# One table that fixes the order of four engines from the last output projection products to the first FFN products, with new PSUM banks

## The chip, the cores and the metric

The kernel runs on one core of a Trainium2 chip. The metric is device time in microseconds (us) for one execution, the median over runs. A core has five instruction streams that work side by side and wait for each other by semaphores: TensorE (PE, matrix products), VectorE (DVE), ScalarE (ACT), GpSimd (POOL) and SyncE (SP), which here issues most of the DMA loads. Products land in PSUM, which this kernel uses as eight banks of 128 x 512 floats; everything else lives in SBUF.

## The reference: what is computed

One layer of a hybrid decoder on x of 1024 tokens by 1024 features, float32:

```python
h = rms_norm(x, mix_norm)
z = h @ w_in                     # split into the parts of two head groups
o_gla = rms_norm(gla_chunked(...), gla_norm) * silu(gr)     # gated linear attention
o_swa = swa_sink_attention(...)                             # sliding window
x = x + concatenate([o_gla, o_swa]) @ w_out
h2 = rms_norm(x, ffn_norm)
u = causal_dwconv(h2 @ w_up, conv_w, conv_b)                # w_up: 1024 x 5632
a, b = split(u, 2)
return x + (silu(a) * b) @ w_down                           # w_down: 2816 x 1024
```

The place of the change is the middle: the output projection with `w_out`, the second RMSNorm, and the first products with `w_up`.

## The kernel before, in words

**Tiles and products.** The 1024 tokens are eight tiles of 128 (t = 0 to 7). Float32 products are made of two parts: every operand is split into a high part (`hi`, a cast by ACT) and a low part (`lo`, the rest, by a subtraction on DVE or POOL; `split`, L102), and three passes (hi·hi, hi·lo, lo·hi) are added up. The output projection and the FFN products use the Winograd form of Strassen's method: the 2 x 2 block product needs seven block products, P1 to P7, instead of eight, at the price of sums and differences of the blocks. One such product, for a pair of tiles (output projection, `o_product`, L829) or for a chunk of 128 columns on each side (FFN, `product`, L977), is 4 x 3 = 12 matmuls of 128 x 128 by 128 x 512 into one bank. P3 of the output projection adds onto the bank of P1, and P4 of the pairs 2 and 3 onto that of P7.

**The stretch of the change.** In order of time:
1. The last gated tiles are transposed into banks called ogt (`gate_tr`, L676, last reader L695); the output projection runs P1 for the pairs i = 0 to 3, then P7 (0, 1), P6 and P5, and then P2, P3, P4 and the rest of P7 mixed. DVE adds each finished bank to the residual tiles `acc` (`o_adds`, L844, its DVE line L852).
2. RMSNorm2 of a tile t whose sums are complete: ACT squares and sums (`norm2_stat`, L214), DVE makes the mean and POOL a power (`rms_scale`, L174); the rows are scaled (`norm2_rows`, L224), either by ACT (scale) and POOL (weights) for the tiles in ROWS_POOL, or by DVE alone in one instruction per half (L235). PE transposes the tile (eight 128 x 128 transposes; L286 for tiles 0 to 3, L253 for 4 to 7). Tiles 0 to 3 are then split into `big` (hi on ACT L290, lo on DVE L298). Tiles 4 to 7 go through `norm2_sums` (L256), which makes the blocks B22, T1, T2, T3 and T4 of the seven products in five sums and splits each.
3. The FFN goes over 22 chunks; chunk c has seven products, with weights that are loaded by SP (`load_side`, L909), combined (`first_sums` L928, `sums` L923) and split (`up_operand`, L934; A11, A12, A22 and S1 to S4 are its operands). The first product needs the high and low parts of tiles 0 to 3, and its matmuls run the eight with high parts first and the four with low parts last. `post` (L1072) puts convolution and gate behind the products; `down_pair` (L1161) multiplies with `w_down`.

**What sets the order.** Every step is registered with a time (`at(time, function, ...)`, `at_us`), the steps are emitted in the order of those times, and a scheduler then orders each engine's instructions by its own estimate. O, TU and the like are starts of stages. Only PE is pinned to the order of emission, by manual dependencies from O to TU + 0.07 (end of the function). On DVE, ACT and POOL the scheduler decides, within what data and buffers demand; a step wrapped in `behind` is put later by it. A norm tile's sums (`norm2_sums`) are one step of about 15 instructions, and so is a tile's scaling.

**PSUM.** Two pools, "a" and "b", of four banks each. `bank` (L55) picks a pool by the beginning of a name, and in turns where no name fits (the ogt banks are such); in a pool the banks go round. A new tile of a bank waits for the last reader of the one before it. All eight FFN banks (`fb0` to `fb3`, `gb0` to `gb3`) are opened at one time, by `open_up_banks` (L750). The FFN product of chunk 0 goes to `gb`, those of the other chunks to `fb`; tiles 3 and 7 of the norm are transposed into `fb2` and `fb3`.

Of the kernel before, what the change touches and what calls it, by code (L numbers as in the profile page):

```python
# [17 lines left out]
P = 128  # L18
# [10 lines left out]
SUMS, EA, EB = 2.01, -25, -14  # L29
# [5 lines left out]
def hymba_layer_kernel(ctx, tc, x, mix_norm, w_in, w_alpha2, b_alpha, gla_norm,  # L35
# [178 lines left out]
    def norm2_stat(t):  # L214
        pn, acc = fin["pn"], fin["acc"][t]
        ss = pn.tile([P, 1], F32, tag="n2ss", name=f"n2ss_{t}", bufs=2)
        if t == 7:
            fin["h", t] = pn.tile([P, D], F32, tag="n2h", name=f"n2h_{t}", bufs=2)
        act.activation(fin["h", t] if t == 7 else early_raw(), acc, AF.Square, accum_out=ss)
        fin["r", t] = rms_scale(ss, D, 1, f"n2{t}", pn, "n2")  # L220

    ROWS_POOL = (0, 1, 2, 4, 5)

    def norm2_rows(t):  # L224
        acc, r = fin["acc"][t], fin["r", t]
# [3 lines left out]
        if t in ROWS_POOL:
            for c in halves:  # L230
                act.activation(h[:, c], acc[:, c], AF.Copy, scale=r[:, 0:1])
                pool.tensor_mul(h[:, c], h[:, c], fin["ffn"][:, c])
            return
        for c in halves:
            dve.scalar_tensor_tensor(h[:, c], acc[:, c], r[:, 0:1], fin["ffn"][:, c],  # L235
                                     op0=ALU.mult, op1=ALU.mult)

    def norm2_tr(t):
        h = fin["h", t]
        if t < 4:  # L240
            b11 = fin["b11"] = fin["pn"].tile([P, 4, 2, P // 2], F32, tag="b11", name=f"b11_{t}", bufs=1)
            tr_hi(t, 0, h, "n2", True)
            act.copy(b11, trs["n2", t, 0])
            tr_lo(t, 0, "n2", True)
            tr_hi(t, 1, h, "n2", True)
            tr_lo(t, 1, "n2", True)
            return
        pbs = fin["pb", t] = []
        for q in range(2):
            pt = bank(f"n2pt_{t}_{q}")  # L250
            for k in range(4):
                c = (q * 4 + k) * P
                pe.transpose(pt[:, k * P:(k + 1) * P], h[:, c:c + P], ident)  # L253
            pbs.append(pt.rearrange("p (k c h) -> p k h c", k=4, h=2))

    def norm2_sums(t):  # L256

        i, ex = t - 4, fin["ex"]
        p0, p1 = fin["pb", t]

        def put(src, dst, eng=dve):
            dst = dst.rearrange("p k r (h c) -> p k r h c", h=2)
            split(src, dst[:, :, 0], dst[:, :, 1], eng)

        b12 = fin["h", t][:, 0:512].rearrange("p (k h c) -> p k h c", k=4, h=2)
        b11 = fin["b11"]
        b21 = big[:, i, 4:8].bitcast(F32).rearrange("p k r (h c) -> p k r h c", h=2)
        act.copy(b12, p0)
        put(p1, big[:, t, 4:8])
        dve.tensor_sub(p1, p1, b12)  # L270
        put(p1, ex[1][:, i])
        dve.tensor_sub(p0, p0, b11)
        put(p0, big[:, t, 0:4])
        dve.tensor_add(p1, p1, b11)
        put(p1, ex[0][:, i])
        dve.tensor_sub(p0, b21[:, :, 0], p1)
        dve.tensor_add(p0, p0, b21[:, :, 1])
        put(p0, ex[2][:, i])
# [550 lines left out]
    def o_product(name, i):  # L829
        onto = "P1" if name in ("P6", "P5", "P3") else "P7" if name == "P4" and i > 1 else None  # L830
        if onto is None:
            psb["o", name, i] = bank(f"o{name}_{i}")
        pb = psb["o", onto or name, i]
        left = o_left(name, i)
        for k in range(4):
            for n, (ra, rb) in enumerate(PASSES):
                pe.matmul(pb, lhsT=left[:, k, ra, :], rhs=two_streams(ow[name, k][:, rb, :]),
                          start=(onto is None and k == 0 and n == 0), stop=(k == 3 and n == 2),
                          skip_group_check=onto is not None)
# [348 lines left out]
    def last_row(t):  # L1188
# [166 lines left out]
    for k in range(4):  # L1355
# [17 lines left out]
    for n, (name, i) in enumerate((("P2", 0), ("P3", 0), ("P4", 0), ("P2", 1), ("P3", 1), ("P7", 2), ("P4", 1), ("P2", 2),  # L1373
                                   ("P3", 2), ("P4", 2), ("P2", 3), ("P3", 3), ("P7", 3), ("P4", 3))):
        u = O + 7 + 0.5 * n
        at(u, o_product, name, i)
        if name in ("P3", "P4"):
            t = i + 4 if name == "P4" else i
            at(u + 0.005, norm2_rows, t)
    for t, n in ((0, 20), (4, 21), (1, 22), (5, 24), (2, 26), (6, 27), (3, 28)):  # L1380
        at(O + 0.5 * n - 0.002, norm2_tr, t)
        if t > 3:
            at(O + 0.5 * n + 0.01, norm2_sums, t)
# [123 lines left out]
```

## Time and profile before

| | us |
|---|---|
| median of 3 runs | 1007.57 (1007.51 to 1008.27) |
| the profiled execution | 1006.84 |
| its span, first to last instruction | 1005.1 |
| PE busy | 975.3 |
| DVE busy | 818.4 |
| POOL busy | 649.2 |
| ACT busy | 505.8 |
| mean granted clock of TensorE | 0.991 |

The span is divided among the engines by "busy"; several are busy at once. A timeline row reads: start, duration, engine, line, operation, output <- inputs, shapes, count, and in brackets the idle time before it with the instruction that ended it. A row of waits reads: who waits <- for whom, total us, times, longest. A row of windows gives for each engine its busy time and its instructions, and then the granted clock of TensorE (1.00 is full speed). Matmuls overlap in the pipe, so that the distance between two starts, and not the duration, is what a product costs.

### The profile page before, as it was taken

To read this page: it belongs to the slowest core of one execution; us is meant where nothing else is said; L and a number is where in the kernel's file an instruction comes from. 1 tells how busy PE (TensorE), PEld (TensorE's weight loads), DVE (VectorE), ACT (ScalarE), POOL (GpSimd) and SP (SyncE) were. 2 spreads that over 40 slices of the span, in tenths; PEclk is the share of its full clock that TensorE was granted. 3 is DMA by queue.
4 is the path that set the end of the run, shared out by engine and by line. 5 is a ranking of instruction groups with operands and counts; after the bars stand their busy time and mean duration, and the time that the engine had idled before them with its cause. 6 is when DMAs were issued, how large, how long until landed. Compare 5 with 4: busy or idle time off the path is not lost.

```text
span 1005.1 us, 13939 instructions
## 1 busy us (share of the span) xinstructions
PE 975.3 (97%) x4915; PEld 842.7 (84%) x4915; DVE 818.4 (81%) x1363; ACT 505.8 (50%) x1039; POOL 649.2 (65%) x542
## 2 busy tenths in 40 slices
PE   8999999999989996999999999999999999999998
PEld 6898878888878774888888888888888888888887
DVE  6877668767573677698998989898989999898986
ACT  5637655445452374455454555445454545455451
POOL 5592232325572654577978788888878797888760
PEclk9999999999998997999999999999999999999999
DMA  6152123032304102202122221212121212222104
GB/s 224 64 157 66 46 64 84 22 85 64 105 1 170 40 0 64 74 32 63 42 64 63 64 64 43 84 43 84 35 72 41 63 42 64 63 64 63 42 22 168
DMA packets 67540, 68.23 MB, mean 68 GB/s; under 512 B 4650, under 2 KB 52237, under 8 KB 67470
## 3 DMA queue, kind: packets, MB, share of 16 engines
q1 hardware_dynamic: 63484, 62.35, 20.1%
q10 hardware_dynamic: 3986, 4.99, 2.1%
q8 instruction: 39, 0.64, 0.3%
q14 instruction: 31, 0.25, 0.1%
HBM read 58.41 MB, written 4.19 MB: 62 GB/s over the span
## 4 chain that ended last, share of the span: by engine, by line
PE 55%; DVE 5%; POOL 2%; issue 1%; DMA 0%; ACT 0%; POOLq 0%; ACTq 0%
PE fb L990 35%; PE dn_P L1171 17%; PE dl L1200 1%; PE fb L1200 1%; DVE n2h L235 1%; PE gb L990 1%; DVE acc L1175 1%; DVE ua L997 0%; DVE ex L107 0%; DMA up<-in_w_up_dram 0%; POOL dw L107 0%; DVE acc L852 0%; DVE big L107 0%; DVE big L298 0%; ACT ex L104 0%
## 5 line engine op out<-in xcount | busy, mean ns | idle before, releaser
L1171 PE MATMUL dn_P<-dw,dg 128*128 128x512 f32 x840 | 205.0, 381 | 1.1 <-DVE acc L1175 0.7
L1175 DVE TENSOR_TENSOR acc<-acc,dn_P 128x1024 f32<-128x1024 f32 x140 | 169.3, 1210 | 31.3 <-PE dn_P L1171 31.2
L1171 PEld LDWEIGHTS dn_P<-dw,dg 128*128 128x128 f32 x840 | 157.2, 189 | 27.1 <-DVE acc L1175 3.2
L107 POOL TENSOR_TENSOR dw<-dn,dw 128x512 fp32r<-128x512 f32 x50 | 64.5, 1290 | 35.8 <-ACT dw L104 35.8
L997 DVE SCALAR_TENSOR_TENSOR ua<-fb,cc,ua 128x511 f32<-128x511 f32 (+1 forms) x84 | 61.9, 739 | 1.2 <-ACT ua L1002 0.8
L990 PE MATMUL fb<-big,A11w 128*128 128x512 f32 x252 | 58.3, 380 | 1.1 <-ACT e L1046 1.1
L990 PE MATMUL fb<-big,S1w 128*128 128x512 f32 x252 | 58.6, 379 | 0.0
L990 PE MATMUL fb<-big,S4w 128*128 128x512 f32 x252 | 58.1, 379 | 0.0
L990 PE MATMUL fb<-big,A12w 128*128 128x512 f32 x252 | 58.1, 379 | 0.0
L990 PE MATMUL fb<-ex,S2w 128*128 128x512 f32 x252 | 58.0, 379 | 0.0
L990 PE MATMUL fb<-ex,A22w 128*128 128x512 f32 x252 | 57.8, 379 | 0.0
L990 PE MATMUL fb<-ex,S3w 128*128 128x512 f32 x252 | 57.8, 379 | 0.0
L522 POOL TENSOR_TENSOR pr<-pr,sm 128x512 f32<-128x512 f32 x16 | 17.3, 1078 | 60.5 <-DVE sm L521 34.6
L1002 ACT ACTIVATE ua<-fb,cc 128x512 f32<-128x512 f32 x42 | 32.7, 778 | 46.3 <-DVE fb L1050 30.0
L990 PEld LDWEIGHTS fb<-big,A11w 128*128 128x128 f32 x252 | 47.5, 189 | 8.2 <-ACT e L1046 1.5
L990 PEld LDWEIGHTS fb<-big,A12w 128*128 128x128 f32 x252 | 47.6, 189 | 6.8
L990 PEld LDWEIGHTS fb<-big,S1w 128*128 128x128 f32 x252 | 47.6, 189 | 6.8
L990 PEld LDWEIGHTS fb<-ex,S3w 128*128 128x128 f32 x252 | 47.6, 189 | 6.8
L990 PEld LDWEIGHTS fb<-big,S4w 128*128 128x128 f32 x252 | 47.6, 189 | 6.8
L990 PEld LDWEIGHTS fb<-ex,A22w 128*128 128x128 f32 x252 | 47.6, 189 | 6.8
L990 PEld LDWEIGHTS fb<-ex,S2w 128*128 128x128 f32 x252 | 47.6, 189 | 6.8
L107 POOL TENSOR_TENSOR A22w<-up,A22w 128x512 fp32r<-128x512 f32 x22 | 30.0, 1363 | 32.0 <-ACT A22w L104 32.0
(487 smaller groups left out, 2573.7 us busy)
## 6 DMA issues: line engine op xcount, KB each, us to landing
up<-in_w_up_dram SPq DMA_DIRECT2D x44, 512.0 KB, 3.8
dn<-in_w_down_dram SPq DMA_DIRECT2D x22, 512.0 KB, 3.4
acc<-in_x_dram SPq DMA_DIRECT2D x8, 512.0 KB, 4.8
out_dram<-acc SPq DMA_DIRECT2D x15, 256.0 KB, 2.1
xt<-in_x_dram SPq DMA_DIRECT2D x7, 512.0 KB, 3.3
vraw<-in_w_in_dram SPq DMA_DIRECT2D x4, 512.0 KB, 4.4
graw<-in_w_in_dram SPq DMA_DIRECT2D x4, 512.0 KB, 3.6
qt<-qt ACTq DMA_DIRECT2D x16, 128.0 KB, 2.2
```

Source lines behind the costliest of these rows:

```text
L107: (eng or pool).tensor_sub(lo, src, hi.bitcast(F32))
L235: dve.scalar_tensor_tensor(h[:, c], acc[:, c], r[:, 0:1], fin["ffn"][:, c], op0=ALU.mult, op1=ALU.mult)
L522: pool.tensor_tensor(pr, pr, den[:, hs].rearrange("p (j o) -> p j o", o=1).broadcast_to((P, 4, P)), ALU.mult)
L990: pe.matmul(pb, lhsT=w[:, ra, k, :], rhs=b_operand(bn, k, rb).rearrange("p t (h c) -> p t c h", h=2), start=(onto is None and i == 0), sto ...
L997: dve.scalar_tensor_tensor(dst, src, w, dst, op0=ALU.mult, op1=ALU.add)
L1002: act.activation(u[:, a:z], y[:, a:z], AF.Identity, bias=b, scale=w2)
L1171: pe.matmul(pb[:, i], lhsT=g[:, ra, c:c + P], rhs=two_streams(w[:, rb, :]), start=(onto is None and n == 0), stop=(n == 2), skip_group_che ...
L1175: dve.tensor_add(acc, acc, pb.rearrange("p i (c h) -> p i h c", h=2))
L1200: pe.matmul(pb[:, c0:c1], lhsT=g[:, ra, (t % 4) * P:(t % 4 + 1) * P], rhs=two_streams(w[:, rb, c0:c1]), start=(ch == NCH - 2 and i == 0), ...
```

## The change

A list of words, `STEPS`, names every step from the fourteen last products of the output projection to the first FFN products, in one order for all engines, and a function `step` carries out each word at O + 7.1 + 0.02 n. Words are: `mm.P2.0` a product, `add.P3.0.1` one addition to `acc`, `stat`, `v`, `pow` the three parts of a tile's norm, `ra` and `r` half a row scaling (ACT's part; POOL's or the whole on DVE), `tr` four transposes, `hi`, `lo`, `h.`, `l.` the halves of a split, `T1` to `T4b` the sums, `wh`, `wl` the halves of a weight's split, `fs` the first sums, `load.1.0` a DMA load, `up` an FFN product, `copy` its copy out of the bank. The composite functions of before (`norm2_stat`, `norm2_rows`, `norm2_tr`, `norm2_sums`, `first_sums`) are taken apart into such steps. The manual dependencies now pin DVE, ACT and POOL too, from O + 7.09 to TU − 0.2.

Other edits: ROWS_POOL is (2, 3, 4, 5, 6) instead of (0, 1, 2, 4, 5). The low parts of A11 and A12 are made on DVE for chunk 0, and on POOL for chunk 1 (before: DVE for both). The names that choose a PSUM pool are others, ogt7 among them (pool "b"). FFN banks are made when first used. Product P7 of pair 2 moves from behind P3 of pair 1 to the front, ahead of P2 of pair 0. Some weights of P3 and P4 are split slightly earlier.

```diff
-SUMS, EA, EB = 2.01, -25, -14
+STEPS = """
+mm.P7.2 mm.P2.0 wh.0.A11 add.P7.2.1 wl.0.A11 mm.P3.0 wh.0.A12 add.P2.0.0 wl.0.A12 mm.P4.0 add.P3.0.1 stat.0
...
+tr.3.1 stat.7 lo.3.0 up.0.P1 T1.6 hi.3.1 v.7 h.T3.6 pow.7 lo.3.1 wh.1.A12 l.T3.6 wh.0.S1 up.0.P2 wl.1.A12
+T2.6 h.T1.6 wh.0.S2 r.7.0 wl.0.S1 b11.3 r.7.1 h.T2.6 copy.0 l.T1.6 up.1.P1 wl.0.S2 wh.0.A22 l.T2.6 wh.0.S3
...
     def bank(name):
-        if "f" in ps:
-            return ps["f"][2 + ps["n"] % 2]
-
-        for which, starts in (("a", ("oP1", "oP4_3", "n2pt_4", "n2pt_5_0", "n2pt_3")),
-                              ("b", ("oP", "n2pt"))):
+        for which, starts in (("a", ("oP1", "n2pt_0_1", "n2pt_4_1", "n2pt_1_0", "oP2_3", "n2pt_2_0", "n2pt_2_1", "n2pt_6_0")),
+                              ("b", ("oP", "n2pt", "ogt7"))):
...
-    ROWS_POOL = (0, 1, 2, 4, 5)
...
+    ROWS_POOL = (2, 3, 4, 5, 6)
...
+    def n2_tr(t, q):
+        pt = up_tile("f", 2 + q) if t in (3, 7) else bank(f"n2pt_{t}_{q}")
...
-    def open_up_banks():
-        for which, key in (("a", "f"), ("b", "g")):
-            ps[key] = [ps[which].tile([P, 512], F32, tag="b", name=f"{key}b{i}") for i in range(4)]
+    def up_tile(key, i):
+        if (key, i) not in ps:
+            ps[key, i] = ps["a" if key == "f" else "b"].tile([P, 512], F32, tag="b", name=f"{key}b{i}")
+        return ps[key, i]
...
+        elif op == "wl":
+            up_operand(*a, dve if a[0] == 0 and a[1] in ("A11", "A12") else pool, (1,))
...
+    for n, word in enumerate(STEPS):
+        at(O + 7.1 + 0.02 * n, step, word)
...
-    at(O + 13.01, load_side, 1, 0)
...
-        if O <= time < TU + 0.07:
+        if O <= time < TU - 0.2:
             for ins in nc.cur_bb.bb.instructions[n:]:
-                if ins.engine == mybir.EngineType.PE:
-                    if last_pe:
+                e = ins.engine
+                if e == mybir.EngineType.PE or time > O + 7.09 and e in PINNED:
+                    if e in last:
```

The order of the instructions, before and after, at three places. First DVE where the last gated tile (ogt7) is read; oP1_3 is the bank of product P1 of pair 3, `qo` and `vg` are the operands in the making. Before:

```order
L690 SCALAR_TENSOR_TENSOR ogt7_3458<-ogt7_3458,glan_118,qo_106 128x512
L107 TENSOR_TENSOR ex1_3142<-ogt7_3458,ex1_3142 128x4x128
L694 TENSOR_TENSOR qo_106<-ogt7_3458,qo_106 128x512
L695 TENSOR_TENSOR vg_1291<-vg_1291,ogt7_3458 128x512
L107 TENSOR_TENSOR ex0_3141<-qo_106,ex0_3141 128x4x128 x3
L852 TENSOR_TENSOR acc1_3144<-acc1_3144,oP1_3_3472 128x512
```

and after:

```order
L719 SCALAR_TENSOR_TENSOR ogt7_3458<-ogt7_3458,glan_118,qo_106 128x512
L119 TENSOR_TENSOR ex0_3141<-qo_106,ex0_3141 128x4x128
L882 TENSOR_TENSOR acc1_3144<-acc1_3144,oP1_3_3472 128x512
L119 TENSOR_TENSOR ex0_3141<-qo_106,ex0_3141 128x4x128
L119 TENSOR_TENSOR ex1_3142<-ogt7_3458,ex1_3142 128x4x128
L723 TENSOR_TENSOR qo_106<-ogt7_3458,qo_106 128x512
L724 TENSOR_TENSOR vg_1291<-vg_1291,ogt7_3458 128x512
```

The addition of P1.3's bank stood behind the last reader of ogt7 (`vg`); now it stands ahead of it, as the product no longer shares a bank with ogt7.

Second, DVE at the entry of the FFN: `n2h_7` are tile 7's scaled rows, `fb2` and `fb3` hold the transposes of tile 3, and `big` takes its low parts. Before:

```order
L176 TENSOR_SCALAR n27v_4101<-n2ss_7_4098 128x1
L298 TENSOR_TENSOR big_65<-fb3_4126,big_65 128x4x128
L235 SCALAR_TENSOR_TENSOR n2h_7_4099<-acc3_3517,n27r_4103,ffn_3595 128x512 x2
L107 TENSOR_TENSOR ex0_3141<-n2pt_6_1_4080,ex0_3141 128x4x128
L276 TENSOR_TENSOR n2pt_6_0_4075<-big_65,n2pt_6_1_4080 128x4x2x64
L298 TENSOR_TENSOR big_65<-fb2_4125,big_65 128x4x128
```

and after:

```order
L327 TENSOR_TENSOR big_65<-fb2_4095,big_65 128x4x128
L287 TENSOR_TENSOR n2pt_6_0_4056<-n2pt_6_0_4056,b11_2_4093 128x4x2x64
L191 TENSOR_SCALAR n27v_4130<-n2ss_7_4112 128x1
L327 TENSOR_TENSOR big_65<-fb3_4106,big_65 128x4x128
L307 TENSOR_TENSOR ex1_3142<-n2pt_6_1_4063,ex1_3142 128x4x128
L289 TENSOR_TENSOR n2pt_6_1_4063<-n2pt_6_1_4063,b11_2_4093 128x4x2x64
L254 SCALAR_TENSOR_TENSOR n2h_7_4111<-acc3_3517,n27r_4133,ffn_3595 128x512 x2
```

Tile 3's low part (`fb2`) was behind tile 7's rows; both of tile 3's low parts now stand ahead of them.

Third, PE at the same place: `gb` and `fb` are the FFN banks, A11w_0 the weight A11 of chunk 0. Before:

```order
L286 MATMUL fb3_4126<-ident_76,n2h_3_4035 128x128 x4
L990 MATMUL gb0_4127<-big_65,A11w_0_3809 128x512 x12
L990 MATMUL gb1_4128<-big_65,A12w_0_3947 128x512 x12
L253 MATMUL fb2_4125<-ident_76,n2h_7_4099 128x128 x4
L253 MATMUL fb3_4126<-ident_76,n2h_7_4099 128x128 x4
L990 MATMUL fb0_4123<-big_65,A11w_1_4069 128x512 x12
L990 MATMUL fb1_4124<-big_65,A12w_1_4072 128x512 x12
L990 MATMUL gb2_4129<-big_65,S4w_0_4220 128x512 x12
```

and after:

```order
L264 MATMUL fb3_4106<-ident_76,n2h_3_4082 128x128 x4
L1033 MATMUL gb0_4115<-big_65,A11w_0_3733 128x512 x12
L1033 MATMUL gb1_4141<-big_65,A12w_0_3749 128x512 x12
L1033 MATMUL fb0_4168<-big_65,A11w_1_4100 128x512 x12
L264 MATMUL fb2_4095<-ident_76,n2h_7_4111 128x128 x4
L264 MATMUL fb3_4106<-ident_76,n2h_7_4111 128x128 x4
L1033 MATMUL gb2_4248<-big_65,S4w_0_4046 128x512 x12
```

The transposes of tile 7 moved behind the first product of chunk 1, and the second product of chunk 1 (A12w_1) to a place four products later.

More of the change, by code (lines that the diff above doesn't have):

```diff
@@ L227, in norm2_rows, with n2_rows @@
+    def n2_rows(t, q, first):
+        acc, r, c = fin["acc"][t], fin["r", t], halves[q]
+        if ("h", t) not in fin:
             fin["h", t] = fin["pn"].tile([P, D], F32, tag="n2h", name=f"n2h_{t}", bufs=2)
         h = fin["h", t]
[L229 to L254, printed above, removed]
@@ L256, in norm2_sums @@
-    def norm2_sums(t):
-        i, ex = t - 4, fin["ex"]
[L259 to L278, printed above, removed]
+        if t not in ROWS_POOL:
+            dve.scalar_tensor_tensor(h[:, c], acc[:, c], r[:, 0:1], fin["ffn"][:, c], op0=ALU.mult, op1=ALU.mult)
+        elif first:
+            act.activation(h[:, c], acc[:, c], AF.Copy, scale=r[:, 0:1])
+        else:
+            pool.tensor_mul(h[:, c], h[:, c], fin["ffn"][:, c])
@@ new lines, in n2_tr, with n2_hi, n2_lo, n2_b11 @@
+    def n2_tr(t, q):
+        pt = up_tile("f", 2 + q) if t in (3, 7) else bank(f"n2pt_{t}_{q}")
+        for k in range(4):
+            c = (q * 4 + k) * P
+            pe.transpose(pt[:, k * P:(k + 1) * P], fin["h", t][:, c:c + P], ident)
+        trs["n2", t, q] = pt.rearrange("p (k c h) -> p k h c", k=4, h=2)
+    def n2_hi(t, q):
+        act.copy(tr_dst(t, q, 0, True), trs["n2", t, q])
+    def n2_lo(t, q):
+        tr_lo(t, q, "n2", True)
+    def n2_b11(t):
+        fin["b11"] = fin["pn"].tile([P, 4, 2, P // 2], F32, tag="b11", name=f"b11_{t}", bufs=1)
+        act.copy(fin["b11"], trs["n2", t, 0])
@@ new lines, in n2_b12, with n2_sum @@
+    def n2_b12(t):
+        fin["b12", t] = fin["h", t][:, 0:512].rearrange("p (k h c) -> p k h c", k=4, h=2)
+        act.copy(fin["b12", t], trs["n2", t, 0])
+    def n2_sum(name, t):
+        p0, p1 = (trs["n2", t, q] for q in range(2))
+        b21 = big[:, t - 4, 4:8].bitcast(F32).rearrange("p k r (h c) -> p k r h c", h=2)
+        if name == "T3":
+            dve.tensor_sub(p1, p1, fin["b12", t])
+        elif name == "T1":
+            dve.tensor_sub(p0, p0, fin["b11"])
+        elif name == "T2":
+            dve.tensor_add(p1, p1, fin["b11"])
+        elif name == "T4a":
+            dve.tensor_sub(p0, b21[:, :, 0], p1)
+        elif name == "T4b":
+            dve.tensor_add(p0, p0, b21[:, :, 1])
@@ L852, in o_adds, with o_add @@
             dve.tensor_add(part, part, halves_of(pb))
-        if name in ("P3", "P4"):
-            norm2_stat(i + 4 if name == "P4" else i)
+    def o_add(name, i, half):
+        onto = "P1" if name == "P3" else "P7" if name == "P4" and i > 1 else name
+        t = i + 4 if name in ("P4", "P7") else i
+        part = fin["acc"][t][:, half * 512:half * 512 + 512].rearrange("p (h c) -> p h c", h=2)
+        dve.tensor_add(part, part, halves_of(psb["o", onto, i]))
     q_count = {}
@@ L952, in up_operand @@
         w = w.rearrange("p r (k n) -> p r k n", k=4)
-        split(src, w[:, 0], w[:, 1], dve if ch < 2 and name[1] == "1" and name[0] == "A" else None)
         blocks["u", ch, name] = w
+        if steps == (0,):
+            blocks["split", ch, name] = src, w[:, 0], w[:, 1]
+            act.copy(w[:, 0], src)
+        else:
+            split(src, w[:, 0], w[:, 1], eng)
     def b_operand(name, k, r):
@@ L1372, in hymba_layer_kernel, with step @@
         at(O + 5 + 0.5 * i, o_product, "P5", i)
[L1373 to L1383, printed above, removed]
+    def step(word):
+        op, *a = word.split(".")
+        a = [int(v) if v.isdigit() else v for v in a]
+        if op == "mm":
+            o_product(*a)
+        elif op == "add":
+            o_add(*a)
+        elif op in ("ra", "r"):
+            n2_rows(*a, op == "ra")
+        elif op in ("stat", "v", "pow", "tr", "hi", "lo", "b11", "b12"):
+            {"stat": n2_stat, "v": n2_v, "pow": n2_pow, "tr": n2_tr, "hi": n2_hi, "lo": n2_lo, "b11": n2_b11, "b12": n2_b12}[op](*a)
+        elif op in ("h", "l"):
+            (n2_part_hi if op == "h" else n2_part_lo)(*a)
+        elif op[0] == "T":
+            n2_sum(op, *a)
+        elif op == "wh":
+            up_operand(*a, None, (0,))
+        elif op == "wl":
+            up_operand(*a, dve if a[0] == 0 and a[1] in ("A11", "A12") else pool, (1,))
+        elif op == "load":
+            load_side(*a)
+        elif op == "fs":
+            if a[0] < 4:
+                first_sum(*a)
+        elif op == "up":
+            product(*a)
+        elif op == "copy":
+            post(a[0], "P1")
+    for n, word in enumerate(STEPS):
+        at(O + 7.1 + 0.02 * n, step, word)
     at(TU - 7.994, mark)
```

89 lines of the change are left out of this document (55 added, 34 removed).

## The prediction

> **What bounds the kernel now.** I read the profile page first: its span, the busy times, and the chain that ended last.
>
> ```profile
> span 1005.1 us, 13939 instructions
> PE 975.3 (97%) x4915; PEld 842.7 (84%) x4915; DVE 818.4 (81%) x1363; ACT 505.8 (50%) x1039; POOL 649.2 (65%) x542
> PE 55%; DVE 5%; POOL 2%; issue 1%; DMA 0%; ACT 0%; POOLq 0%; ACTq 0%
> ```
>
> TensorE is the bound: busy for 975.3 us of 1005.1, and the largest share of the chain. The change removes no product, so all it can win is PE's idle time and PE's slow time. The profiled execution took 1006.84 us in all, 0.73 below the median of the runs (1007.57): I make the sum against the profiled one and add 0.73 at the end. A difference of 0.2% (2 us) is about what a measurement of this kernel can tell from none.
>
> The waits of PE, up to 320 us and then from 320 to 452 us (us in total, times, longest), say where the idle time in reach lies.
>
> ```profile
> PE oP L837 <- DVE vg L695: 4.9, 1, 4.9
> ```
> ```profile
> PE gb L990 <- DVE big L298: 6.3, 1, 6.3
> PE fb L286 <- DVE n2h L235: 1.6, 1, 1.6
> PE n2pt L286 <- POOL n2h L232: 1.6, 2, 1.1
> PE n2pt L253 <- DVE n2pt L276: 1.3, 2, 0.8
> PE fb L990 <- ACT e L1046: 1.1, 1, 1.1
> ```
>
> Two waits stand out: A, 4.9 us before the product P1.3 of the output projection, and B, 6.3 us inside the FFN's first product. The rest of the second list is a dozen short ones.
>
> **Stage A (296 to 307 us).** The timeline of PE, then of DVE, then windows (busy time of PE, PEld, DVE, ACT, POOL, then PEclk, the granted clock):
>
> ```profile
> 296.44 0.60 PE L679 MATMUL ogt<-ident,gs 128*128 128x128 f32 x4
> 301.90 5.46 PE L837 MATMUL oP<-ex,big 128*128 128x512 f32 x12 [4.86 <-DVE vg L695]
> 307.15 5.62 PE L837 MATMUL oP<-oP7w,big 128*128 128x512 f32 x24
> 312.60 10.52 PE L837 MATMUL oP<-oP6w,ex 128*128 128x512 f32 x48
> ```
> ```profile
> 295.42 0.68 DVE L695 TENSOR_TENSOR vg<-vg,ogt 128x512 f32<-128x512 f32 x1
> 301.07 0.68 DVE L695 TENSOR_TENSOR vg<-vg,ogt 128x512 f32<-128x512 f32 x1
> ```
> ```profile
> 302.00:304.00 2.00, 2.00 (x5) 1.64 (x6) 0.00 (x0) 0.45 (x1) 0.00 (x0) 0.50 0.00 0
> 304.00:307.10 3.10, 3.10 (x8) 2.43 (x8) 1.72 (x3) 1.49 (x4) 0.00 (x0) 0.50 0.00 0
> ```
>
> P1.3 shares a PSUM bank with ogt7, the transposes of the last gated tile, and so starts only after ogt7's last reader (DVE, 301.07 to 301.75). Having stood for 4.86 us, PE then has a clock of 0.50, and the 12 matmuls take 307.15 − 301.90 = 5.25 us. At full clock a product takes 424.59 − 422.00 = 2.59 (below).
>
> After the change ogt7 has a bank of pool "b". The bank of P1.3 then holds ogt6 before it, whose last reader is the first of the two DVE rows: done at 296.1. So P1.3 starts when the four transposes are through (half of the 0.86 that eight take, below: 296.44 + 0.43 = 296.9) and ends at 299.5, where P7.0 follows. Before, P7.0 starts at 307.15: **7.65 us** less, 5.0 of it the wait and 2.65 the clock. Bounds: 0, if something else releases P1.3 as late; 7.65 is all there is. P7, P6 and P5 follow without a wait of their own. The DVE chain of ogt7 (split, qo, vg) now stands behind two more instructions, but nobody needs it before P6.3, the last 12 of the 48 matmuls at 312.60, and P5 behind them. The loads and splits of the weights in between follow from PE's progress and shift with it. I take 7.65.
>
> **Stage B (333 to 437 us).** PE, then DVE, then windows:
>
> ```profile
> 333.32 2.88 PE L837 MATMUL oP<-oP2w,big 128*128 128x512 f32 x12
> ...
> 337.17 2.64 PE L837 MATMUL oP<-ex,big 128*128 128x512 f32 x11 [0.76 <-POOL ex L107]
> ...
> 358.74 1.10 PE L286 MATMUL n2pt<-ident,n2h 128*128 128x128 f32 x8
> 359.60 2.84 PE L837 MATMUL oP<-ex,big 128*128 128x512 f32 x12
> ...
> 384.27 1.32 PE L286 MATMUL fb<-ident,n2h 128*128 128x128 f32 x8 [1.64 <-DVE n2h L235]
> 385.61 1.99 PE L990 MATMUL gb<-big,A11w 128*128 128x512 f32 x8
> 393.94 2.07 PE L990 MATMUL gb<-big,A11w 128*128 128x512 f32 x4 [6.34 <-DVE big L298]
> 395.81 4.76 PE L990 MATMUL gb<-big,A12w 128*128 128x512 f32 x12
> 400.40 1.04 PE L253 MATMUL fb<-ident,n2h 128*128 128x128 f32 x8
> ...
> 422.00 2.75 PE L990 MATMUL gb<-ex,A22w 128*128 128x512 f32 x12
> 424.59 2.75 PE L990 MATMUL fb<-ex,S3w 128*128 128x512 f32 x12
> ...
> 436.61 2.86 PE L990 MATMUL fb<-big,A11w 128*128 128x512 f32 x12 [1.10 <-ACT e L1046]
> ```
> ```profile
> 382.17 0.68 DVE L107 TENSOR_TENSOR ex<-n2pt,ex 128x512 fp32r<-128x512 f32 x1
> 382.76 0.68 DVE L107 TENSOR_TENSOR big<-n2pt,big 128x512 fp32r<-128x512 f32 x1
> 383.36 1.52 DVE L235 SCALAR_TENSOR_TENSOR n2h<-acc,n23r,ffn 128x512 f32<-128x512 f32 x2
> 388.68 3.41 DVE L235 SCALAR_TENSOR_TENSOR n2h<-acc,n27r,ffn 128x512 f32<-128x512 f32 x2
> 393.21 0.68 DVE L298 TENSOR_TENSOR big<-fb,big 128x512 fp32r<-128x512 f32 x1
> ```
> ```profile
> 372.00:384.00 12.00, 8.14 (x41) 6.03 (x40) 12.00 (x20) 9.31 (x19) 8.61 (x8) 1.00 0.28 79
> 385.60:387.60 2.00, 1.99 (x8) 1.43 (x8) 2.00 (x4) 1.58 (x3) 0.00 (x0) 1.00 0.29 77
> 396.00:398.00 2.00, 2.00 (x7) 1.53 (x6) 0.00 (x0) 0.58 (x1) 0.00 (x0) 0.50 0.00 0
> ```
>
> The FFN's first product stops after 8 of 12 matmuls: the low part of tile 3 (393.21) stands on DVE behind tile 7's row scaling (388.68, 3.41 us for two halves). The 16 matmuls after that stop then take 400.40 − 393.94 = 6.46 us at half clock instead of 16 × 0.216 = 3.46: 3.0 more.
>
> *Ceiling.* From P2.0 at 333.32 to the end of product P4 of chunk 0 (424.59) both orders have 25 products and 16 groups of four transposes: 25 × 2.59 + 16 × 0.43 = 71.6 us of work, so at best 404.95. That would gain 19.6.
>
> *What still waits.* I walked the new order of the engines, with 0.60 for a DVE step (382.17 to 382.76), 0.76 or 1.70 for half a row on DVE (383.36, 388.68), and a POOL step, an ACT step and a load by these rows (two of the timelines, one of the page's DMA issues):
>
> ```profile
> 375.89 1.28 POOL L107 TENSOR_TENSOR S4w<-up,S4w 128x512 fp32r<-128x512 f32 x1 [2.09 <-ACT S4w L104]
> 378.71 0.62 ACT L104 CAST S3w<-up 128x512 fp32r<-128x512 f32 x1
> up<-in_w_up_dram SPq DMA_DIRECT2D x44, 512.0 KB, 3.8
> ```
>
> (times on before's scale, stage A's shift left out.)
> - P7.2 takes the slot at 333.32. It covers the 0.76 us wait of P3.0, whose weight is ready at 337.1; P3.0 now starts at 338.5. Uncovered, it costs 0.8.
> - P4.3 ends at 374.9 and the transposes of tile 3 at 375.8, against 385.6 before. Tile 3's rows go to POOL (ready 375.15, needed 375.35) and tile 7's stay on DVE behind tile 3's low parts.
> - The first FFN product starts at 375.95; tile 3's low part is ready at 376.75, its ninth matmul needs it at 377.7. So the 6.34 us and the clock loss go. Then P2 of chunk 0 and P1 of chunk 1 run to 383.75. Tile 7's rows need 3.4 us on DVE beside POOL's splits and end at 382.8. These two products cover them.
> - What is late next is tile 7: its B22 is cast late, and the product S4 waits 0.75 us for the high and 0.55 for the low part. With about 0.45 of smaller ones, P4 of chunk 0 ends at 404.95 + 1.75 = 406.7.
> - P1 of chunk 2 (436.61) follows this end by 12.0 us in both, as it hangs on ACT's edge copy behind the same chain, and the program behind it is the same. The gain is kept.
>
> So stage B gives 424.59 − 406.7 = **17.9**. Bounds: 19.6 (no wait) and about 10 (the stop at the FFN's entry remains in part, first rival). The edits without a price of their own (split of the scale into two steps, banks made on demand, pins on DVE, ACT and POOL) emit the same instructions; the pins cost only through the order, which I have walked. The load of chunk 1's first half is held behind tile 3's statistic on SP; it lands about 373.8, and the ACT cast that uses it stands right ahead of tile 3's high part at 374.7: 0.9 us of slack, and each us beyond it is a us of PE.
>
> The sum: 7.65 + 17.9 = 25.55. A dozen places of the walk have under 1 us of slack; I take off 0.55 for them. Gain 25.0: 1006.84 − 25.0 = 981.84 for a profiled execution, and 1007.57 − 25.0 = **982.5** as median.
>
> [...] Row 385.60:387.60 shows that after 1.64 us of standing the clock is still 1.00; rows 302.00 and 396.00 show 0.50 after 4.86 and 6.34. [...]
>
> Row 388.68 shows 1.70 us for half a row on DVE beside POOL work, row 383.36 shows 0.76. [...]
>
> **The rivals.**
> 1. *DVE is the bound at the FFN's entry.* From the first statistic to tile 7's last sum DVE has 74 steps, some 44 us of work in 47.5. If it runs 3 to 4 us late, PE stops again, inside the first product or at tile 7. For it: DVE's 12.00 of 12.00 busy in 372:384. Against it: the steps are ordered by need now. Price: 4.5 us of stop and 3.0 of clock, gain 25.0 − 7.5 = 17.5: **990.1**.
> 2. *The bank was not what held P1.3* (the change does not do what it says). The releaser is inferred; if a weight or an operand came as late, stage A gains nothing. Against it: L695 ends at 301.75 and P1.3 starts at 301.90. Gain 17.35: **990.2**.
> 3. *Lockstep, slower than before.* With four engines pinned into one order, a step whose input is late holds all that stands behind it on its engine, and the other engines through that: the wait appears at each product. Price: n us at each of the 25 products. Before, single waits of this kind are 0.2 to 1.6 us, at only some ten places. It decides from 1.0 us at each product (25 us, the whole gain); at 1.2, and with the gain of 25.0, 982.6 + 30 = **1012.6**. Against it: by the walk, nearly every step has its input early.
>
> **How the numbers follow.** Forecast (980 to 986): 0.72. Rival 1: 0.12. Rival 2: 0.08. Both of these at once, near 997.7: 0.03. No change, by waits that make up for the gain: 0.02. Rival 3: 0.03. The low end is the ceiling, 7.65 + 19.6 = 27.25, 1007.57 − 27.25 = 980.3, less what the short waits after 424 may add: 979.5. The high end takes in rivals 1 and 2: 990.5. Faster by over 0.2%: 0.95, within: 0.02, slower: 0.03.
>
> **What the profile after would show.** Right: no wait of P1.3 and its 12 matmuls in 2.6 us, P7.0 near 299.5; no wait over 1 us between P2.0 and the FFN's first products, PEclk 1.00 from 290 to 430; the first FFN product near 375.95 − 7.65 = 368.3 and P1 of chunk 2 near 411. Wrong: a wait of P1.3 on anything at 301; a stop of several us at the FFN's entry with a clock near 0.5 behind it; P1 of chunk 2 later than 415; or a longer rest of the program, which I take to be unchanged.

## The result and the profile after

| | before | after |
|---|---|---|
| median, us | 1007.54 (1005.97 to 1008.27, 4 runs) | 982.71 (981.06 to 983.13, 4 runs) |
| ratio | | 0.9753 (95% interval 0.9736 to 0.9769) |
| profiled execution, us | 1006.84 | 981.06 |
| its span, us | 1005.1 | 979.3 |

The forecast was 982.5 with a range of 979.5 to 990.5. Each later comparison has its own runs of the kernel before beside it (medians 1006.3 to 1006.8), so for every experiment the difference to its own "before" is given; for the change it is −24.83 us. By the intervals such a difference is uncertain by some 2 us.

The page of the kernel after: span, busy times, and the chain that ended last.

```profile
span 979.3 us, 13946 instructions
PE 966.4 (99%) x4915; PEld 839.2 (86%) x4915; DVE 813.9 (83%) x1361; ACT 505.1 (52%) x1039; POOL 651.6 (67%) x544
PE 82%; DVE 8%; POOL 3%; DMA 3%; issue 2%; ACT 2%; ACTq 0%; DVEq 0%; POOLq 0%; SPq 0%
```

PE is busy for 99% of the span. Its busy time itself fell by 8.9 us with the same 4915 matmuls. Some 5.9 us of that are matmuls which no longer run at a clock of 0.50 (2.9 behind the first stop, 3.0 behind the second); the rest was not traced. Of the waits of PE between 312 and 430 us two are left, where the list of before (320 to 452 us, the same work) had nine:

```profile
PE fb L1033 <- ACT e L1089: 1.0, 1, 1.0
PE gb L1033 <- ACT big L303: 0.8, 1, 0.8
```

The timeline of PE after, at the places that were shown of before: P1.3 and P7.0; the first product of the stretch that the table orders (P7.2 now); tile 3's transposes and the first FFN products; product S4 of chunk 0; the end of P4 of chunk 0 (the start of the next product, 399.08); and P1 of chunk 2.

```profile
296.99 2.84 PE L867 MATMUL oP<-ex,big 128*128 128x512 f32 x12
299.66 5.34 PE L867 MATMUL oP<-oP7w,big 128*128 128x512 f32 x24
...
325.56 2.75 PE L867 MATMUL oP<-oP7w,big 128*128 128x512 f32 x12
...
367.07 1.31 PE L264 MATMUL fb<-ident,n2h 128*128 128x128 f32 x8
368.35 2.86 PE L1033 MATMUL gb<-big,A11w 128*128 128x512 f32 x12
371.04 2.75 PE L1033 MATMUL gb<-big,A12w 128*128 128x512 f32 x12
...
378.04 2.86 PE L1033 MATMUL gb<-big,S4w 128*128 128x512 f32 x12 [0.78 <-ACT big L303]
...
399.08 2.75 PE L1033 MATMUL fb<-ex,S3w 128*128 128x512 f32 x12
...
410.73 2.86 PE L1033 MATMUL fb<-big,A11w 128*128 128x512 f32 x12 [1.00 <-ACT e L1089]
```

Both stops are gone. P1.3 follows the transposes at once and its 12 matmuls take 299.66 − 296.99 = 2.67 us (before 5.25). The first FFN product runs its 12 without a stop. On DVE, the low parts of tile 3 (L327) now stand ahead of tile 7's rows (L254):

```profile
368.48 0.68 DVE L327 TENSOR_TENSOR big<-fb,big 128x512 fp32r<-128x512 f32 x1
...
370.13 0.69 DVE L327 TENSOR_TENSOR big<-fb,big 128x512 fp32r<-128x512 f32 x1 [0.30 <-ACT big L268]
...
371.93 2.76 DVE L254 SCALAR_TENSOR_TENSOR n2h<-acc,n27r,ffn 128x512 f32<-128x512 f32 x2
```

The windows after (busy time of PE, PEld, DVE, ACT and POOL, then the granted clock) show the entry of the FFN with the clock at 1.00, PE nearly full, and DVE nearly full too:

```profile
364.00:376.00 12.00, 11.94 (x61) 10.21 (x60) 11.66 (x19) 11.36 (x22) 10.06 (x9) 1.00 0.12 34
```

Where the time came from, by the starts of the same PE work in the two profiled executions:

| | before | after | earlier by | gained in the stretch |
|---|---|---|---|---|
| first P1 product | 288.59 | 288.78 | −0.19 | |
| P7.0 | 307.15 | 299.66 | 7.49 | 7.68 |
| first product behind P5 | 333.32 | 325.56 | 7.76 | 0.27 |
| end of P4 of chunk 0 | 424.59 | 399.08 | 25.51 | 17.75 |
| P1 of chunk 2 | 436.61 | 410.73 | 25.88 | 0.37 |
| end of the span | 1005.1 | 979.3 | 25.8 | −0.1 |

The 0.27 behind P7.0 is clock too: before, it was 0.50 until 307.69, and so for the first 0.54 us of P7.

### The profile page after: what moved, and what is told of

The parts are those of the page before. It is cut to its first block, busy times and chain, and to the rows that moved or that the text cites. A ratio compares the mean times of both kernels' runs of the same rounds, so it can differ in the third digit from the quotient of the medians.

```text
span 979.3 us, 13946 instructions
## 1 busy us (share of the span) xinstructions
PE 966.4 (99%) x4915; PEld 839.2 (86%) x4915; DVE 813.9 (83%) x1361; ACT 505.1 (52%) x1039; POOL 651.6 (67%) x544
## 4 chain that ended last, share of the span: by engine, by line
PE 82%; DVE 8%; POOL 3%; DMA 3%; issue 2%; ACT 2%; ACTq 0%; DVEq 0%; POOLq 0%; SPq 0%
PE fb L1033 36%; PE dn_P L1214 18%; PE oP L867 7%; PE dr L389 4%; PE dg L389 4%; PE dv L389 3%; PE pv L575 1%; PE dl L1243 1%; PE fb L1243 1%; DMA qraw<-in_w_in_dram 1%; DVE ua L1040 1%; PE go L685 1%; PE ga L676 1%; PE ppt L560 1%; PE go L688 1%
## 5 line engine op out<-in xcount | busy, mean ns | idle before, releaser
L1085 ACT COPY ca<-fb 128x512 f32<-128x512 f32 x62 | 36.3, 585 | 28.6 <-PE fb L1033 28.6
```

What stands on the lines that cost most here:

```text
L1085: act.copy(dst, pb)
```

## The experiments

The theory: the gain is two things, a shared bank (stage A, some 7.65 us) and the order of the engines up to the FFN (stage B, some 18). The rivals: another cause of the wait at P1.3; DVE as the bound of the FFN's entry; a lockstep in which any late input of a pinned order stops PE.

### The bank, undone and alone

The changed kernel with `ogt7` out of pool b:

```diff
-                              ("b", ("oP", "n2pt", "ogt7"))):
+                              ("b", ("oP", "n2pt"))):
```

> The changed kernel, with ogt7 taken out of pool b's names, so that it shares a bank with P1.3 again; PE's order and the table stay. If the shared bank is what held P1.3 (the prediction): P1.3 waits 4.9 us again on DVE's last reader of ogt7, its 12 matmuls take 5.2 us at a clock of 0.50, and the median is 982.7 + 7.65 = 990.4. If something else held it, and the table's order brought the gain of that stage: no wait, 982.7.

Measured: 990.28 us (988.7 to 990.54), −16.31 to its before, ratio 0.9836 (0.9816 to 0.9855). PE's timeline:

```profile
302.66 4.96 PE L867 MATMUL oP<-ex,big 128*128 128x512 f32 x12 [4.86 <-DVE vg L724]
307.46 5.34 PE L867 MATMUL oP<-oP7w,big 128*128 128x512 f32 x24
```

The wait is back to the hundredth (4.86), the 12 matmuls take 4.80 us, and 8.5 of the 24.83 us are lost (7.6 by the two profiled executions). And the kernel before with that edit alone:

```diff
-                              ("b", ("oP", "n2pt"))):
+                              ("b", ("oP", "n2pt", "ogt7"))):
```

> The kernel before, with nothing changed but ogt7 put into pool b. If the bank holds P1.3: P1.3 starts at 297 and P7.0 at 299.6 instead of 307.15, all behind it is 7.65 us earlier, with the stop of 6.3 us at the FFN's entry as before: 1007.5 - 7.65 = 999.9. If loads or weight splits behind it do not follow PE (they were hidden by the stop): some of the 7.65 comes back as new waits between 312 and 345, and the median is between 1001 and 1007.

Measured: 998.65 us (998.49 to 1000.17), −7.94, ratio 0.9926 (0.9906 to 0.9945).

```profile
297.62 2.84 PE L837 MATMUL oP<-ex,big 128*128 128x512 f32 x12
300.29 5.34 PE L837 MATMUL oP<-oP7w,big 128*128 128x512 f32 x24
```

So the shared bank held P1.3, and one word in a list of names is worth about 8 us, with or without the table. The rival (another releaser, or loads behind it that come too late) falls: P3.0's wait behind it is 0.5 us, where it was 0.8.

The same run shows something at the FFN's entry that matters below. The stop of 1.64 us at tile 3's transposes left the clock at 1.00 in the kernel before. Here a stop of the same 1.64 us is followed by a clock of 0.50, and the eight matmuls behind it take 3.63 us instead of 1.99 (the two windows are 3.41 us long):

```profile
376.74 1.32 PE L286 MATMUL fb<-ident,n2h 128*128 128x128 f32 x8 [1.64 <-DVE n2h L235]
378.07 3.63 PE L990 MATMUL gb<-big,A11w 128*128 128x512 f32 x8
386.41 2.08 PE L990 MATMUL gb<-big,A11w 128*128 128x512 f32 x4 [4.71 <-DVE big L298]
```
```profile
374.86:378.27 3.41, 1.75 (x11) 1.04 (x10) 3.41 (x6) 2.45 (x5) 1.28 (x2) 1.00 0.99 278
378.27:381.68 3.41, 3.41 (x8) 2.17 (x7) 3.27 (x7) 2.46 (x5) 1.12 (x2) 0.50 0.10 27
```

The slow matmuls only fill time that PE would have waited anyway: the stop inside the product is 4.71 us instead of 6.34.

### DVE's order at the FFN's entry, turned round

The changed kernel with tile 7's rows, and three steps of tile 6, ahead of tile 3's low parts on DVE; the other engines keep their order:

```diff
-tr.3.1 stat.7 lo.3.0 up.0.P1 T1.6 hi.3.1 v.7 h.T3.6 pow.7 lo.3.1 wh.1.A12 l.T3.6 wh.0.S1 up.0.P2 wl.1.A12
-T2.6 h.T1.6 wh.0.S2 r.7.0 wl.0.S1 b11.3 r.7.1 h.T2.6 ...
+tr.3.1 stat.7 hi.3.1 v.7 h.T3.6 pow.7 r.7.0 r.7.1 T1.6 l.T3.6 T2.6 lo.3.0 up.0.P1 lo.3.1 wh.1.A12 wh.0.S1
+up.0.P2 wl.1.A12 h.T1.6 wh.0.S2 wl.0.S1 b11.3 h.T2.6 ...
```

> The changed kernel, with only DVE's order turned round at the FFN's entry: tile 7's two row scalings and three of tile 6's steps ahead of tile 3's low parts, as before. If DVE's order there was the stop of 6.3 us: PE stops after 8 matmuls of the first FFN product for about 5.5 us, its clock falls to 0.50 for some 6 us, which costs 3 more, and the wait of 0.8 at tile 7 goes; 982.7 + 7.7 = 990.4. If DVE has room to make it up, because tile 7 is then ready earlier: under 985.

Measured: 988.17 us (987.63 to 988.97), −18.42, ratio 0.9817 (0.9795 to 0.984): 6.4 of the gain lost. PE, and DVE's row scaling:

```profile
375.13 2.07 PE L1033 MATMUL gb<-big,A11w 128*128 128x512 f32 x4 [3.98 <-DVE big L327]
377.00 4.50 PE L1033 MATMUL gb<-big,A12w 128*128 128x512 f32 x12
381.33 2.75 PE L1033 MATMUL fb<-big,A11w 128*128 128x512 f32 x12
```
```profile
371.27 1.42 DVE L254 SCALAR_TENSOR_TENSOR n2h<-acc,n27r,ffn 128x512 f32<-128x512 f32 x2 [0.66 <-POOL n27r L196]
```

The stop is back, 3.98 us instead of the 5.5 expected, as the rows took 1.42 us where most of them ran ahead of POOL's splits (2.76 in the change, among the splits). The one split that began beside them, at 371.98, took 1.83 us instead of 1.28. The 16 matmuls behind it take 6.20 us for 3.46: 2.74 to the clock. 3.98 + 2.74 = 6.7. DVE did not make it up, although tile 7 was ready earlier. One part of the expectation was wrong: the wait of 0.8 us at S4 stayed.

Then only the two row scalings ahead:

```diff
+tr.3.1 stat.7 hi.3.1 v.7 h.T3.6 pow.7 r.7.0 r.7.1 lo.3.0 up.0.P1 T1.6 lo.3.1 wh.1.A12 l.T3.6 wh.0.S1
+up.0.P2 wl.1.A12 T2.6 h.T1.6 wh.0.S2 wl.0.S1 b11.3 h.T2.6 ...
```

> As the run before it, but only the two row scalings stand ahead of tile 3's low parts: the stop should be about 2.9 us (the rows start at 370.45 behind the power, take 1.8 to 2.7 us, the low part 0.6, needed at 370.1). [...] If any stop of 2 us or more halves the clock: 982.7 + 5.1 = 987.8.

Measured: 985.38 us (985.25 to 987.46), −21.21, ratio 0.9795 (0.9775 to 0.9815): 3.6 lost. PE's timeline, then windows:

```profile
374.94 1.85 PE L1033 MATMUL gb<-big,A11w 128*128 128x512 f32 x4 [2.20 <-DVE big L327]
376.58 3.77 PE L1033 MATMUL gb<-big,A12w 128*128 128x512 f32 x12
380.18 2.75 PE L1033 MATMUL fb<-big,A11w 128*128 128x512 f32 x12
```
```profile
374.00:375.00 1.00, 0.06 (x1) 0.06 (x1) 1.00 (x3) 0.01 (x1) 1.00 (x1) 1.00 0.00 0
375.00:376.00 1.00, 1.00 (x3) 0.84 (x4) 1.00 (x3) 0.48 (x1) 1.00 (x2) 0.60 0.00 0
376.00:377.00 1.00, 1.00 (x3) 0.74 (x3) 1.00 (x3) 0.63 (x2) 0.94 (x2) 0.50 0.00 0
```

Behind this stop of 2.20 us the clock is 0.50: the 16 matmuls take 5.24 us, 1.78 too many. Here the clock falls only when the stop is over and PE works again (1.00 at 374, 0.60 at 375); in the stops of 3.98 us and more it fell while PE still stood (in the run above at 373.69, 1.44 us before PE went on).

### Two edits without the table

The kernel before with ogt7 in pool b, and tile 7's rows on DVE behind tile 3's first low part (a manual dependency):

```diff
             tr_lo(t, 0, "n2", True)
+            if t == 3:
+                ahead.update((ins.engine, ins.name) for ins in nc.cur_bb.bb.instructions)
...
-            at(u + 0.005, norm2_rows, t)
+            at(O + 14.0002 if t == 7 else u + 0.005, *((behind, norm2_rows) if t == 7 else (norm2_rows,)), t)
```

> The kernel before with two edits and no table: ogt7 in pool b, and on DVE tile 7's rows pinned behind the low part of tile 3 that the first FFN product needs. If two places made most of the time: the stop of 4.7 us that was left with the bank alone falls to about 1.5 and the clock stays at 1.00, so 998.7 - 3.2 - 3 = 992.5. If tile 7's rows, which are then later, only move the stop behind the second product: 997 to 999.

Measured: 994.72 us (993.11 to 995.9), −12.10, ratio 0.9875 (0.9856 to 0.9895).

```profile
384.39 2.07 PE L993 MATMUL gb<-big,A11w 128*128 128x512 f32 x4 [2.88 <-DVE big L301]
386.26 3.51 PE L993 MATMUL gb<-big,A12w 128*128 128x512 f32 x12
```

Half of the gain. The stop shrank to 2.88, not to 1.5, and the clock still fell with it (0.59 from 384 to 386). The expectation took its 3.2 us off the stop of 4.7 of the run with the bank alone, which slow matmuls ahead of it had shortened by 1.6; off the full 6.34 it would have come to 3.1. The other waits of before in this stretch stand as they did (0.2 to 1.6 us each). The rest, 12.7 us, is in the main what the table does beyond these two places: the rest of this stop and the short waits. Some of it is not: in the profiled execution (995.81) PE also lost some 2 us near 150 us (last section), and of the other three one is as long (995.9), while two took 993.1 and 993.6.

### The table without its pins

```diff
-    last, PINNED = {}, (mybir.EngineType.DVE, mybir.EngineType.Activation, mybir.EngineType.Pool)
+    last, PINNED = {}, ()
```

> The changed kernel with its table, but only PE is pinned to it; DVE, ACT and POOL are ordered by the scheduler again, out of the same small steps (its order differs in some 70 places on DVE; tile 3's low parts still stand ahead of tile 7's rows). If the small steps and the banks bring the gain: within 2 us of 982.7. If the pins do: waits of PE come back between 330 and 390, by what the kernel before had there beside its big stop, some 7 us: 990.

Measured: 989.31 us (988.48 to 990.57), −17.51, ratio 0.9827 (0.9808 to 0.9845): 7.3 lost. The three longest of the seven waits of PE, and the timeline at tile 3:

```profile
PE fb L264 <- POOL n2h L258: 2.6, 2, 2.1
PE n2pt L264 <- DVE n2h L254: 1.4, 1, 1.4
PE fb L1033 <- DVE ex L307: 0.6, 1, 0.6
```
```profile
372.11 0.66 PE L264 MATMUL fb<-ident,n2h 128*128 128x128 f32 x4 [2.06 <-POOL n2h L258]
373.33 1.11 PE L264 MATMUL fb<-ident,n2h 128*128 128x128 f32 x4 [0.57 <-POOL n2h L258]
374.10 4.10 PE L1033 MATMUL gb<-big,A11w 128*128 128x512 f32 x12
378.04 2.75 PE L1033 MATMUL gb<-big,A12w 128*128 128x512 f32 x12
```

The pins do some 40% of stage B (7.3 of 17.75 us; the scheduler's order of some FFN products differs in this run too, and belongs to the 7.3). Between the two edits (−12.10) and this run (−17.51) lie 5.4 us for the small steps, the other banks and the other shares of work among the engines; these were not taken apart. Tile 3's low parts stand ahead of tile 7's rows here too, but tile 3's rows on POOL come 2.06 us late, and the product behind takes 3.94 us for 2.59.

### One cast moved: what a late input costs in a fixed order

The changed kernel with ACT's cast of chunk 1's first weight ahead of tile 3's row scaling:

```diff
-... lo.2.0 mm.P4.3 ra.3.0 lo.2.1
+... lo.2.0 mm.P4.3 wh.1.A11 ra.3.0 lo.2.1
...
-... tr.3.0 wh.1.A11 add.P4.3.0 hi.3.0
+... tr.3.0 add.P4.3.0 hi.3.0
```

> The changed kernel with one step of the table moved: the ACT cast of chunk 1's first weight, whose load lands at about 366.3, stands ahead of tile 3's row scaling (364.33) instead of four casts later. Lockstep theory: ACT stands for about 2 us, tile 3's rows, transposes and the FFN's entry are as much later (they have no slack), PE waits 2 to 2.5 us at tile 3's transposes; 982.7 + 2.3 = 985.0, and about 1.7 more (986.7) if the clock falls, as it did after the stop of 2.2. If the other engines make it up: 982.7.

Measured: 986.99 us (985.34 to 988.3), −19.83, ratio 0.9799 (0.978 to 0.9818): 5.0 lost. ACT, then PE:

```profile
367.62 0.62 ACT L995 CAST A11w<-up 128x512 fp32r<-128x512 f32 x1 [2.50 <-DMA up<-in_w_up_dram]
```
```profile
370.26 0.66 PE L264 MATMUL fb<-ident,n2h 128*128 128x128 f32 x4 [2.35 <-POOL n2h L258]
371.49 1.11 PE L264 MATMUL fb<-ident,n2h 128*128 128x128 f32 x4 [0.58 <-POOL n2h L258]
372.26 4.12 PE L1033 MATMUL gb<-big,A11w 128*128 128x512 f32 x12
376.21 2.75 PE L1033 MATMUL gb<-big,A12w 128*128 128x512 f32 x12
```

ACT stands 2.50 us for a load, POOL gets tile 3's rows later, PE stands 2.35, and the next product takes 3.95 us for 2.59. The lockstep is real: a wait goes through three engines nearly undiminished, and the clock adds 1.4. The change does not suffer from it because in the order of its table this input comes in time.

### Three small ones

Product P7.2 back behind P3.1 (in the table `mm.P7.2` and its addition moved):

> The changed kernel with product P7.2 back in its old place behind P3.1. If it is the cover of P3.0's weight, as the prediction says: P3.0 waits 0.5 to 0.8 us, the clock stays, 982.7 + 0.7 = 983.4, which is less than the runs can tell, but the waits of PE show it. If the weight is ready in time: no wait.

Measured: 983.05 us (982.35 to 983.79), −23.77, ratio 0.9761 (0.9745 to 0.9776). The wait that P7.2 covers is there, 0.36 us instead of the 0.76 of before:

```profile
329.26 2.64 PE L867 MATMUL oP<-ex,big 128*128 128x512 f32 x11 [0.36 <-POOL ex L119]
```

Tile 3's rows on DVE (`ROWS_POOL` without 3, and no `ra.3` in the table):

> The changed kernel with tile 3's rows on DVE (as in the kernel before) instead of ACT and POOL. If DVE is near its bound at the FFN's entry, the two halves (1.4 us or more) push tile 3's low part from 368.5 to 370 and tile 7's rows to 376: a wait of 0.5 us in the first product and of about 1 at tile 7's transposes, 982.7 + 1.5 = 984.2, with the clock at 1.00 as no single wait is over 1.6. If DVE has room there: no new wait, 982.7, or less, since tile 3's rows are then ready earlier than POOL makes them.

Measured: 982.3 us (981.75 to 983.21), −23.98, ratio 0.9763 (0.975 to 0.9777): no difference that the runs can tell. Tile 3's transposes wait 0.54 us, the first FFN product and tile 7's transposes wait for nothing new. The trace shows a small price: from P7.3 (360.62; 360.14 in the change) to P1 of chunk 2 (411.88; 410.73) it takes 0.7 us more. So DVE could take 1.4 us more at nearly no loss, at a place where it is busy for 97% (11.66 of 12.00).

The cast of tile 7's block B22 earlier on ACT, against the last wait of 0.78:

```diff
-... tr.7.0 copy.1 tr.7.1 b12.7 up.1.P2 l.T4.5 h.B22.7 T1.7 h.T4.6 l.B22.7
+... tr.7.1 tr.7.0 h.B22.7 copy.1 b12.7 up.1.P2 l.T4.5 l.B22.7 T1.7 h.T4.6
```

> The changed kernel with tile 7's second transposes and the cast of its block B22 moved ahead of two copies on ACT (and its low part ahead of T1 on DVE), to take the wait of 0.78 us away that is left at product S4 of chunk 0. If that wait hangs on ACT's order alone: it falls to 0.1 or 0.2, and 0.6 us less in all, 982.1, which the profile shows and the runs can hardly tell; the steps behind it, moved by the scheduler, may give it back at the edge copy of chunk 1 (1.0 us before P1 of chunk 2), then 982.7.

Measured: 982.15 us (981.64 to 983.25, 5 runs), −24.13, ratio 0.9761 (0.9748 to 0.9775): no gain.

```profile
PE fb L1033 <- ACT e L1089: 1.0, 1, 1.0
PE fb L1033 <- POOL S4w L119: 0.6, 1, 0.6
PE gb L1033 <- ACT ex L303: 0.4, 1, 0.4
PE gb L1033 <- ACT big L303: 0.2, 1, 0.2
```

The wait fell from 0.78 to 0.24, so it did hang on ACT's order (a copy that waits for the end of a product stood ahead of the cast); but waits of 0.42 and 0.64 came in behind it. No version here is faster than the change by more than the runs can tell.

## Why the prediction was right

The sum was 25.0 from 1007.57; the medians differ by 24.83, the profiled executions by 25.78.

- **Stage A**, 7.65 forecast, 7.68 by the trace. The inferred releaser was the true one: both directions of the bank experiment show it. P7.0 was forecast at 299.5 and stands at 299.66. The sum left out the 0.27 us behind P7.0, where the clock was still 0.50.
- **Stage B**, 17.9 forecast, 17.75 by the trace. The FFN's entry was forecast at 368.3 (368.35), P1 of chunk 2 near 411 (410.73). The mechanism is as forecast, but that the sum comes out so close is in part luck: two terms were each off by about 1 us and cancel. Of the 1.75 us of waits that the walk left, 0.75 at the high part of B22 came (0.78); the 0.55 at its low part and the 0.45 of smaller ones did not show as waits. And the 25 products with their transposes took longer than the 71.6 of the ceiling: from 325.56 to 399.08 it is 73.52 us, which without the wait of 0.78 leaves 72.7. The largest piece is tile 3's transposes, 1.28 us instead of 0.86: their rows on POOL ended at 367.68 (forecast 375.15 − 7.65 = 367.50, with 0.2 of slack), and PE's weight load waited some 0.3 us for them. Tile 3's low part ended at 369.16 and was needed at 368.35 + 8 × 0.216 = 370.08: 0.9 of slack, as worked out.
- **The 0.55 taken off for tight places** was not needed by the profiled executions (25.55 without it, against 25.78). Against the medians (24.83) the sum with it is the closer one, but the two differ by less than the runs can tell.
- **Tile 7's rows beside POOL**: taken at 3.4 us, they took 2.76. Mostly ahead of POOL's splits they took 1.42 (both runs with the rows first). Behind the two products it made no difference. Before, beside POOL's work, they took 3.41. In the change the two POOL splits that ran beside them (372.41 and 374.11) took 1.73 and 1.74 us, and the one ahead and the one behind 1.28.
- **The load of chunk 1** was the step with the wrong size: 0.9 us of slack were worked out, and there was hardly any. Where ACT waited for it, the load ended 4.68 us after tile 3's statistic (367.62, with the statistic's end at 362.94), not the 3.8 of the page's median; moved to the change's times, where the statistic ends at 362.27, that is 366.95 (an estimate; the landing in the change itself was not read), and ACT casts at 366.99. By this the order was right by a hair, and here too the forecast had luck.
- **Rival 1** (DVE bound) is half true. The order of DVE at the entry is worth 6.4 us, but DVE is no hard bound there: it takes 1.4 us more at a price of 0.7 us by the trace, which the runs cannot tell.
- **Rival 3** (lockstep) has its mechanism shown, and not its condition: one late input cost 5.0 us. Five of that size would add up to the whole gain; the change has none.
- **The clock's price** for a short stop was not shown by the profile before: it has a clock of 1.00 behind 1.64 us and of 0.50 behind 4.86 and 6.34, and no stop of PE between 1.7 and 4.86. In the run with the two edits a stop of 2.88 us cost 4.6 with its slow matmuls (1.76).

## What to carry to other kernels

A product that waits may wait for a bank and not for its data: compare the releaser with what last used the output's buffer. Where several engines hand work to each other in steps of half a microsecond, the order within each engine is worth as much as the work itself; smaller steps in one list gain more when the queues are made to follow it (7.3 us here). In these runs the stops of PE of 2.00 to 6.34 us had 1.35 to 3.00 us of slow matmuls behind them, and one of 1.64 us had 1.64 (bank alone) or none (before): the price of such a stop is the stop and the slow matmuls.

## What the runs showed of the hardware

**In these runs TensorE's clock went by stretches of 3.41 us, and not by the length of a stop alone.** The profiles of eight of the kernels above have places with a clock of 0.50. Read in windows of 0.1 us, the clock falls and comes back at the times of this table. "Idle ahead" is PE's idle time in the 3.41 us that end at the fall; "lost" is what the matmuls took beyond their time at full clock.

| stop, us | kernel and place | clock 0.50 from, to | that is | idle ahead, us | lost, us |
|---|---|---|---|---|---|
| 1.64 | bank alone, tile 3's transposes | 378.27, 381.68 | 3.41 | 1.66 | 1.64 |
| 2.00 | two edits, near 150 us | 152.27, 155.68 | 3.41 | 2.00 | 1.69 |
| 2.06 and 0.57 | no pins | 373.26, 376.68 | 3.42 | 2.55 | 1.35 |
| 2.20 | rows first, short | 375.21, 378.62 | 3.41 | 2.20 | 1.78 |
| 2.35 and 0.58 | cast early | 371.45, 374.86 | 3.41 | 2.75 | 1.36 |
| 2.50 | rows first, short, near 150 us | 153.34, 156.75 | 3.41 | 1.99 | 1.69 |
| 2.88 | two edits | 384.37, 387.79 | 3.42 | 2.86 | 1.76 |
| 3.98 | rows first, long | 373.69, 380.52 | 6.83 | 2.54 | 2.74 |
| 4.71 | bank alone | 385.09, 391.92 | 6.83 | 3.40 | 2.80 |
| 4.86 | before, stage A | 300.86, 307.69 | 6.83 | 3.41 | 2.93 |
| 4.86 | bank undone | 300.15, 306.98 | 6.83 | 2.34 | 2.21 |
| 6.34 | before, stage B | 389.61, 399.85 | 10.24 | 2.01 | 3.00 |

Every slow stretch of the table lasts once, twice or three times 3.41 us. Where one trace has two, their beginnings lie whole numbers of 3.413 us apart: 88.75 (26 times), 6.82 (2), 221.87 (65) and 232.10 (68). So in these runs the clock changes on a grid of 3.41 us that runs on through the execution. Counted on this grid, it fell behind stretches in which PE was idle for 1.66 us or more, and stayed at 1.00 behind ones with up to 1.72, which puts the edge at about half of the stretch (an estimate from these two numbers). It came back behind the first stretch in which PE was idle for 0.07 us or less, and not behind ones with 0.92 or more.

This fits the stop of 1.64 us that goes both ways. In the kernel before it lay across a border of the grid, with 1.51 us of idle time in one stretch, and the clock stayed; with the bank alone all of it lay in one stretch. The longest stop that left the clock at 1.00 in one of these eight traces is 1.73 us (cast early, near 150 us), the shortest that halved it 1.64. PE was busy for up to 1.75 us of a stretch behind which the clock fell (bank alone, 374.86 to 378.27), and stops of 1.64 to 2.88 us were enough. The grid began 0.5 to 3.2 us behind the span's start in these traces; nothing here shows a way to choose its place.

**One execution lost 2 us by the same edge.** PE waits near 150 us in every profile, for 1.3 to 1.7 us in ten of the twelve and with a clock of 1.00. In the profiled execution of the run with the short stop it waited 2.5 us:

```profile
PE dg L389 <- ACT vg L920: 2.5, 1, 2.5
```

The clock was 0.50 for 3.41 us behind it, and the first P1 product started at 291.18 us, where it starts at 288.78 in the change. That execution took 987.46 us at a mean clock of 0.997, the other three of the same kernel 985.25 to 985.41 at 0.998. The run with the two edits has the same, with a wait of 2.00 us. Why the wait itself differs is not shown. By these clocks the wait was over the edge in one execution of four (an estimate; the other three have no trace), and the times lie 2 us apart. The change's own runs look like it: 981.06 has a mean clock of 1.000, the three others (982.3 to 983.13) have 0.998, which is what one slow stretch of 3.41 us in 981 would give (an estimate), but no trace shows it.
